# Forming every weight's low part on VectorE instead of sharing the work with GpSimd

## The chip, the cores and the metric

The kernel runs on one core of a Trainium2 chip. The metric is the device time of one execution in microseconds (us); of several executions the median is taken. The names in the profile are PE (TensorE, matrix products), PEld (its weight loads), DVE (VectorE), ACT (ScalarE), POOL (GpSimd) and SP (SyncE, which issues the weight transfers).

## The reference

Two layers of a hybrid diffusion backbone run over 256 latent and 256 context tokens of width 1024. Cut to what matters:

```python
for l in range(2):
    xn, hn = adaln(x, norm1[l], ...), adaln(h, norm1[l], ...)      # latent, context
    u = [xn; hn] @ w_in[l]                     # one projection, feeds three mixers
    ya = latent_attention(u); yb = window_attention(u); yc = gated_deltanet(u)
    y = merge(gates, ya @ w_a, yb @ w_b, yc @ w_c) @ w_out[l]
    x = x + m[2] * y
    a, b = split(dwconv(adaln(x, norm2[l], ...) @ ffn_up[l], ffn_conv[l]))
    x = x + m[5] * ((silu(a) * b) @ ffn_down[l])
    # the context stream h likewise, in layer 0 only: the last layer drops it after the mixers
out = rmsnorm(x, norm_f)
```

All inputs and outputs are fp32.

## The kernel before

**Products in three parts.** Each fp32 product is made of three reduced-precision (fp32r) products. A weight tile comes as `raw` from HBM; ACT casts it to the high part `wh` (line 194), and the low part `wl = raw - wh` is formed by a subtraction (`split_L`, line 184). `mm3` (lines 204 to 206) then adds `wh*xh`, `wh*xl` and `wl*xh` in PSUM. So the product of line 206 is the first that needs `wl`. Activations are split in the same way by `split` (ACT cast, line 199; DVE subtraction, line 200).

**Tiles and buffers.** `linear` goes over units of 256 output columns; each unit takes weight tiles of 128 x 1024 (four blocks of 128 rows by 256 columns; 128 x 768 at the end of `ffn_down`). There are three `raw`, three `wh` and four `wl` buffers. PSUM tiles are tagged `mm` (three) and `g` (five). With both streams a product has 512 columns, in the last layer after the mixers 256.

**Who forms `wl`.** `split_L` adds a share `lpool` to a running sum and gives the subtraction to GpSimd each time the sum reaches 1, else to VectorE. `lpool` is 1.0 from the first weights to the end of layer 0's first projections, 0 in the DeltaNet stages, and 0.33 from the attentions through the merges, the output projection and the feed-forwards. So there GpSimd forms each third low part.

**Other work on the two engines.** In a feed-forward, each pair of 128-wide blocks goes: ACT scales the product (1606), DVE adds the two shifted terms of the convolution (1609, 1611), ACT applies silu to the first block (1623), POOL multiplies the two (1627), and `split` makes the parts that `ffn_down` reads (199, 200). Residuals are added by DVE (1566). A norm squares on ACT (368), sums on POOL (or DVE at the end, 372), sums over partitions on PE (383), takes the power -1/2 on POOL (348), spreads it on PE (391) and scales on DVE and ACT (404, 410, 411).

**Order.** Each engine and each DMA queue runs its own instructions in order. The order is made when the program is built, by a scheduler that takes the instructions by priority and by readiness under its own costs; semaphores are added by it. The kernel steers it with generators (`run_gen`, `fill`), which interleave projections with the DeltaNet chain.

Of the kernel before, what the change touches and what calls it, by code (L numbers as in the profile page):

```python
# [5 lines left out]
F32 = mybir.dt.float32  # L6
# [3 lines left out]
ALU = mybir.AluOpType  # L10
# [19 lines left out]
def make_consts():  # L30
# [56 lines left out]
MARK = None  # L87
P = dict(pw=4,
    l1={}, s2=(2, 1, 2, 0), pe=(0.0, 0.1, 0.0, 0.0), ov=0, np=(0.1, 0.0, 0.25, 0), ly=2, qs=(0, 4), dec1=3.0, dec2=4.0, sol1=4.2, sol2=4.0,
    sol3=1.0, sol4=2.0, sca=(1.0, 2.0), scb=(1.0, 2.0), scc=(1.0, 2.0), lpg=0.0, lpn=0.33, cap=12.0, sl=(0.3, 0.3, 0.5, 0.1), modc=(4.0, 0.9),  # L90
    lag=(0, 0, 2, 4, 5), nmod=(2, 5), hk=(5, 12), f0=(1.0, 1.6, 1.0, 1.0, 1.5, 1.0, 1.0), f1=(1.0, 1.0, 1.0, 0.3, 1.0, 1.0, 0.3), lat=1.0,
    bx=4, wd=0, dc=1, gk=(0, 0), hpe=60, w_t=5, w_k=3, w_s=0, w_r=1.5, w_n=3, w_o=4.0, nr=3, nh=3, nl=4, nb2=7, st=0, ab=(0.0, 0.0, 0.0, 0.0),
    st2=6, lp0=1.0, lpb=0.33, bge=2, hpa=40, hpn=0, hpk=40, hpv=40)

_INS = ["x", "c", "ctx", "c_ctx", "w_mod", "b_mod", "norm1", "norm2", "w_in", "mla_q_norm", "mla_kv_norm",
        "w_uq", "w_ukv", "swa_sink", "gdn_conv", "gdn_a_log", "gdn_dt_bias", "gdn_norm",
# [38 lines left out]
class Kernel:  # L135
# [40 lines left out]

    def split_L(self, out, x, h):

        self.lacc += self.lpool
        e = self.nc.vector  # L180
        if self.lacc >= 1.0:
            self.lacc -= 1.0
            e = self.nc.gpsimd
        e.tensor_tensor(out=out, in0=x, in1=h.bitcast(F32), op=ALU.subtract)  # L184

    def load_split(self, srcs, shape):

# [228 lines left out]
    def setup(self):  # L416
        nc, i = self.nc, self.ins
        self.cst = self.per.tile([128, CONSTS.shape[1]], F32, name="cst")
        nc.sync.dma_start(out=self.cst[:, :130], in_=i["consts"][:, :130])
        ident = self.con("ident")  # L420
        crow, cs = self.b2([16, 128]), self.b2([16, 128])
        nc.scalar.dma_start(out=crow[0:8, :], in_=i["c_ctx"].rearrange("(k p) -> k p", p=128))
        nc.scalar.dma_start(out=crow[8:16, :], in_=i["c"][0].rearrange("(k p) -> k p", p=128))
        self.x0 = [self.b4([128, D]) for _ in range(4)]
        for n in (2, 3, 0, 1):
            nc.sync.dma_start(out=self.x0[n], in_=i["x" if n // 2 else "ctx"][0, n % 2 * 128:n % 2 * 128 + 128, :])
        nc.scalar.activation(out=cs, in_=crow, func=AF.Silu)
        self.cT = self.per.tile([128, KD, 32], F32, name="cT")
        nc.vector.memset(self.cT, 0.0)
        pc = self.ps([128, T], "g")  # L430
        nc.tensor.transpose(pc[:, :16], cs, ident[:16, :16])
        nc.vector.tensor_copy(self.cT[:, :, 0:2].rearrange("p k s -> p s k"), pc[:, :16].rearrange("p (s k) -> p s k", k=KD))
        self.vec, self.fcv, self.mod, self.AB = [], [], [], []
        for l in range(DEPTH):
            self.vec.append(self.per.tile([128, NVEC], F32, name=f"vec{l}"))
            self.fcv.append(self.per.tile([128, FC_ROWS], F32, name=f"fcv{l}"))
            self.mod.append(self.per.tile([128, 6, KD, 2], F32, name=f"mod{l}"))
            self.AB.append(self.per.tile([128, 2, KD, 2], F32, name=f"AB{l}"))
        self.lpool = self.P["lp0"]
        m = self.m0 = self.modulation_first()  # L440
        for _ in range(self.P["st"]):
            next(m)
        v = self.load_vectors(0)
        next(v)
        self.load_x()
        for _ in range(4 - self.P["st"]):
            next(m)
        next(v)
        next(m)
        self.v0 = v  # L450
# [848 lines left out]
    def layer(self, l):  # L1299
# [89 lines left out]
        def finish(*gens):  # L1389
            self.gsync()  # L1390
            self.finish(*gens)
# [12 lines left out]

        self.XT, self.N, self.qk, self.oacc, self.qr, self.St = {}, {}, {}, {}, {}, None
        self.mark(f"gproj_{l}")
        if l:
            self.lpool = self.P["lpg"]
        self.gdn_alloc()
        self.gates = gates() if self.P["gk"][l] else None  # L1410
        self.run_gen(self.gdn_part(l, X, 1, lambda: self.norm1(l, 1)))
# [6 lines left out]
        mods = [self.modulation(l, 1), self.modulation(l, 2)]  # L1418
        self.gates = self.gates or gates()
        self.queue = [gq, gv, gkv, self.gates]  # L1420
        self.lpool = self.P["lpg"]
        spill = self.dram.tile([128, KD, T], F32, name=f"spill{l}")
        for j in range(2):
            nc.sync.dma_start(out=spill[:, j * 4:j * 4 + 4], in_=self.xT[j])
# [30 lines left out]
        chain(go1)  # L1455
        self.mark(f"mlaprep_{l}")
        finish(gsq, gmq)
        self.lpool = self.P["lpn"]
        yc = A["zs"]
        qh, kh, vt = A["qh"], A["kh"], A["vt"]  # L1460
        self.mark(f"mla_{l}")
# [117 lines left out]
                self.mod_A(l, 1)  # L1579
            yield from self.norm_mod(xT, self.AB[l][:, 1], self.mod[l][:, 3], *self.X2, s)  # L1580

        self.lpool = self.P["lpb"]
        self.run_gen(self.linear(i["w_out"][l], 0, KD, 0, D, (mH, mL), residual(2, 0, True), cols=lambda _: slice(0, n),
                                 split=None if last else 3, hook=lambda: norm2(0)))
        if last:
# [10 lines left out]
        for half in range(2):  # L1596
            aH, aL = [], []
            for a in (aH, aL):
                for al, m_ in ((self.s8, 4), (self.s8, 4), (self.b4, 2), (self.b4, 1)):
                    t = al([128, m_, T], F32R)  # L1600
                    a += [t[:, k] for k in range(m_)]
            f0 = half * 11

            def conv(y, p, cs, o):
                c0, c1 = cs.start // S, cs.stop // S
                nc.scalar.activation(out=y[:, cs], in_=p[:, cs], func=AF.Identity, scale=fc[:, 44 + o:45 + o])
                yv = y.rearrange("p (s j) -> p s j", s=2)[:, c0:c1]
                pv = p.rearrange("p (s j) -> p s j", s=2)[:, c0:c1]
                nc.vector.scalar_tensor_tensor(out=yv[:, :, 1:], in0=pv[:, :, :S - 1], scalar=fc[:, o:o + 1],
                                               in1=yv[:, :, 1:], op0=ALU.mult, op1=ALU.add)  # L1610
                nc.vector.scalar_tensor_tensor(out=yv[:, :, :S - 1], in0=pv[:, :, 1:], scalar=fc[:, 88 + o:89 + o],  # L1611
                                               in1=yv[:, :, :S - 1], op0=ALU.mult, op1=ALU.add)
                return y

            for f in range(f0, f0 + 11, 2):
                nf = min(2, f0 + 11 - f)
                av = {}

                def eva(t, p, cs):
                    if t not in av:  # L1620
                        av[t] = self.b2([128, T])
                    y = conv(av[t], p, cs, f + t)
                    nc.scalar.activation(out=y[:, cs], in_=y[:, cs], func=AF.Silu)

                def evb(t, p, cs):
                    y = conv(self.b2([128, T]), p, cs, f + t + 22)
                    nc.gpsimd.tensor_tensor(out=y[:, cs], in0=y[:, cs], in1=av[t][:, cs], op=ALU.mult)  # L1627
                    self.split(aH[f + t - f0][:, cs], aL[f + t - f0][:, cs], y[:, cs])

                if nf == 1:  # L1630
                    self.run_gen(self.linear(i["ffn_up"][l], 0, KD, (f * 128, (f + 22) * 128), 256, X,
                                             lambda t, p, cs: evb(0, p, cs) if t else eva(0, p, cs), cols=c_o))
                    continue
                self.run_gen(self.linear(i["ffn_up"][l], 0, KD, f * 128, nf * 128, X, eva, cols=c_o,
                                         split=0 if f == 0 and not last else None, hook=lambda: norm2(1)))
                self.lpool = self.P["lpn"]
                self.run_gen(self.linear(i["ffn_up"][l], 0, KD, (f + 22) * 128, nf * 128, X, evb, cols=c_o))
            if last and half:
                self.final_load()
            self.lpool = self.P["lpb"] if half else self.P["lpn"]  # L1640
            self.run_gen(self.linear(i["ffn_down"][l], f0, 11, 0, D, (aH, aL), residual(5, None, half == 1), cols=c_o,
                                     split=3 if half == 1 and not last else None, hook=lambda: self.norm1(l + 1, 0)))
        while self.bg:
# [10 lines left out]
    def run(self):  # L1654
        nc, tc, i = self.nc, self.tc, self.ins
        self.NS8, self.NS4, self.NB2, self.NSM = 8, 9, self.P["nb2"], 32
        self.NRAW, self.NWH, self.NWL, self.NMM = self.P["nr"], self.P["nh"], self.P["nl"], 3
        self.lpool, self.lacc = 0.0, 0.0
        self.queue, self.bg, self.gcount, self.bg_every, self.credit, self.modcost, self.gates, self.wait, self.sq_last, self.bgx, self.unit, self.wide = [], [], 0, 3, 0.0, 4.0, None, 0.0, None, None, 0, False
        with tc.tile_pool(name="per", bufs=1) as self.per, tc.tile_pool(name="sb", bufs=1) as self.pool, \  # L1660
                tc.tile_pool(name="psum", bufs=1, space=PSUM) as self.psum, \
                tc.tile_pool(name="dram", bufs=1, space=DRAM) as self.dram:
            self.setup()
            for l in range(DEPTH):
                self.layer(l)
            self.mark("final")
            self.final()
# [62 lines left out]
```

## Time and profile before

| | us |
|---|---|
| median of 3 runs | 1794.27 |
| lowest and highest | 1787.89, 1797.77 |
| the profiled execution | 1803.63 |
| its span, first to last instruction | 1801.8 |

The profiled execution lies 9.4 us above the median, and 1.8 us of it lie outside the span. The mean granted clock of TensorE over the span is 0.962 of full speed. In the rows, times are us from the span's start unless marked ns; `x` is a count; a bracket or the last column tells how long the engine had been idle and what ended the wait.

### The profile page before, as it was taken

How to read it: one execution, taken by the hardware profiler on the slowest of the kernel's cores; microseconds unless marked ns; L12 is line 12 of the kernel's file. 1: busy time of each engine (PE TensorE's matmuls, PEld its weight loads, DVE VectorE, ACT ScalarE, POOL GpSimd, SP SyncE). 2: the span in 40 equal slices, each digit the busy share in tenths (PEclk: the TensorE clock that was granted, in tenths of full speed). 3: DMA queues.
4: the chain of work that ended last, by engine and by line, in shares of the span. 5: the costliest groups of instructions: out<-in, count | busy, mean ns of one | idle time of the engine just before them, and what ended most of it. 6: DMA issues, size and time to landing. Idle time of an engine off the chain costs nothing. (4 is left out here: it accounts for less than half of the span.)

```text
span 1801.8 us, 31553 instructions
## 1 busy us (share of the span) xinstructions
PE 1689.5 (94%) x12723; PEld 1371.2 (76%) x12723; DVE 1082.6 (60%) x2089; ACT 767.2 (43%) x1371; POOL 456.0 (25%) x351
## 2 busy tenths in 40 slices
PE   7989888999999999999999999989889899999997
PEld 4768766776557888668888888768777668989996
DVE  2896594565775433445334434798886866466573
ACT  3644411234665233334324333565433564554453
POOL 3130501122100423112212222032412403434241
PEclk9999997998999999999999999999989899989998
DMA  9323325333134543853333345334441214745553
GB/s 341 114 80 108 96 88 164 68 85 101 45 117 155 184 136 109 311 170 94 97 103 93 94 155 155 94 88 131 100 100 30 81 59 138 239 122 169 182 171 111
DMA packets 216944, 228.75 MB, mean 127 GB/s; under 512 B 51228, under 2 KB 195422, under 8 KB 215646
## 3 DMA queue, kind: packets, MB, share of 16 engines
q1 hardware_dynamic: 211582, 220.11, 39.9%
q10 hardware_dynamic: 4928, 6.56, 1.0%
q8 instruction: 100, 1.64, 0.4%
q14 instruction: 46, 0.38, 0.1%
q0 software_dynamic: 288, 0.06, 0.0%
HBM read 213.85 MB, written 11.80 MB: 125 GB/s over the span
## 5 line engine op out<-in xcount | busy, mean ns | idle before, releaser
L194 ACT CAST wh<-raw 128x1024 fp32r<-128x1024 f32 (+2 forms) x294 | 298.4, 1016 | 412.8 <-PE mm L205 212.8
L184 DVE TENSOR_TENSOR wl<-raw,wh 128x1024 fp32r<-128x1024 f32 (+1 forms) x224 | 280.3, 1252 | 201.9 <-ACT wh L194 182.3
L204 PE MATMUL mm<-xnh,wh 128*128 128x512 f32 (+2 forms) x1072 | 381.6, 357 | 5.6 <-ACT wh L194 2.4
L206 PE MATMUL mm<-xnh,wl 128*128 128x512 f32 (+2 forms) x1072 | 376.1, 353 | 2.6 <-DVE wl L184 1.3
L205 PE MATMUL mm<-xnl,wh 128*128 128x512 f32 (+2 forms) x1072 | 375.5, 351 | 0.7 <-DVE xnl L411 0.6
L184 POOL TENSOR_TENSOR wl<-raw,wh 128x1024 fp32r<-128x1024 f32 (+2 forms) x70 | 162.5, 2322 | 448.7 <-ACT wh L194 419.2
L204 PEld LDWEIGHTS mm<-xnh,wh 128*128 128x128 f32 (+1 forms) x1072 | 206.4, 193 | 39.6 <-issue 7.6
L206 PEld LDWEIGHTS mm<-xnh,wl 128*128 128x128 f32 (+1 forms) x1072 | 205.7, 192 | 33.1 <-issue 2.9
L205 PEld LDWEIGHTS mm<-xnl,wh 128*128 128x128 f32 (+1 forms) x1072 | 206.4, 193 | 28.1 <-DVE xnl L411 2.2
L204 PE MATMUL g<-xnh,wh 128*128 128x256 f32 (+1 forms) x496 | 167.9, 340 | 1.4 <-ACT xnh L410 1.4
L206 PE MATMUL g<-xnh,wl 128*128 128x256 f32 (+1 forms) x496 | 166.6, 337 | 2.1 <-POOL wl L184 2.1
L205 PE MATMUL g<-xnl,wh 128*128 128x256 f32 (+1 forms) x496 | 166.3, 337 | 0.2 <-DVE xnl L411 0.2
L204 PE MATMUL mm<-s,wh 128*128 128x256 f32 (+1 forms) x458 | 151.0, 331 | 2.3 <-ACT s L199 1.7
L206 PE MATMUL mm<-s,wl 128*128 128x256 f32 (+1 forms) x458 | 150.8, 330 | 1.7 <-POOL wl L184 1.1
L205 PE MATMUL mm<-s,wh 128*128 128x256 f32 (+1 forms) x458 | 150.5, 329 | 0.1
L204 PEld LDWEIGHTS g<-xnh,wh 128*128 128x128 f32 x496 | 94.7, 192 | 15.4 <-issue 3.7
L205 PE MATMUL g<-s,wh 128*128 128x512 f32 (+1 forms) x304 | 103.6, 341 | 2.4 <-DVE s L200 2.4
L204 PE MATMUL g<-s,wh 128*128 128x512 f32 (+1 forms) x304 | 104.1, 342 | 1.3 <-ACT s L199 1.3
L206 PEld LDWEIGHTS g<-xnh,wl 128*128 128x128 f32 x496 | 94.6, 191 | 13.2 <-POOL wl L184 2.9
L206 PE MATMUL g<-s,wl 128*128 128x512 f32 (+1 forms) x304 | 103.3, 340 | 0.0
L205 PEld LDWEIGHTS g<-xnl,wh 128*128 128x128 f32 x496 | 94.8, 192 | 10.0 <-DVE xnl L411 0.8
L1627 POOL TENSOR_TENSOR b<-b,b 128x512 f32<-128x512 f32 (+1 forms) x44 | 54.6, 1240 | 170.9 <-DVE b L1611 149.6
(286 smaller groups left out, 2865.9 us busy)
## 6 DMA issues: line engine op xcount, KB each, us to landing
raw<-in_w_in_dram SPq DMA_DIRECT2D x92, 512.0 KB
raw<-in_ffn_up_dram SPq DMA_DIRECT2D x80, 512.0 KB
s<-in_w_mod_dram SPq DMA_DIRECT2D x64, 512.0 KB
raw<-in_w_mod_dram SPq DMA_DIRECT2D x32, 512.0 KB
raw<-in_ffn_down_dram SPq DMA_DIRECT2D x32, 512.0 KB
raw<-in_w_out_dram SPq DMA_DIRECT2D x16, 512.0 KB
raw<-in_ffn_down_dram SPq DMA_DIRECT2D x16, 384.0 KB
spill<-s SPq DMA_DIRECT2D x4, 1024.0 KB
```

The source lines that it names most:

```text
L184: e.tensor_tensor(out=out, in0=x, in1=h.bitcast(F32), op=ALU.subtract)
L194: nc.scalar.copy(H, raw)
L204: mm(ps, lhsT=wH, rhs=xH, start=start, stop=False)
L205: mm(ps, lhsT=wH, rhs=xL, start=False, stop=False)
L206: mm(ps, lhsT=wL, rhs=xH, start=False, stop=stop)
L1627: nc.gpsimd.tensor_tensor(out=y[:, cs], in0=y[:, cs], in1=av[t][:, cs], op=ALU.mult)
```

## The change

`split_L` always takes VectorE, and the shares and their running sum are gone. Nothing else is edited. The diff, without the lines of the parameter table:

```diff
     def split_L(self, out, x, h):
 
-        self.lacc += self.lpool
-        e = self.nc.vector
-        if self.lacc >= 1.0:
-            self.lacc -= 1.0
-            e = self.nc.gpsimd
-        e.tensor_tensor(out=out, in0=x, in1=h.bitcast(F32), op=ALU.subtract)
+        self.nc.vector.tensor_tensor(out=out, in0=x, in1=h.bitcast(F32), op=ALU.subtract)
...
-        self.lpool = self.P["lp0"]        # setup: 1.0
-        if l:
-            self.lpool = self.P["lpg"]    # gproj of layer 1: 0.0
-        self.lpool = self.P["lpg"]        # after the first projections: 0.0
-        self.lpool = self.P["lpn"]        # attentions, merges: 0.33
-        self.lpool = self.P["lpb"]        # output projection: 0.33
-                self.lpool = self.P["lpn"]
-            self.lpool = self.P["lpb"] if half else self.P["lpn"]
-        self.lpool, self.lacc = 0.0, 0.0
```

## Rows read from the trace of the kernel before

**Rows 1.** The page's first part: busy time, share of the span, instructions

```profile
PE 1689.5 (94%) x12723; PEld 1371.2 (76%) x12723; DVE 1082.6 (60%) x2089; ACT 767.2 (43%) x1371; POOL 456.0 (25%) x351
```

**Rows 2.** Instructions grouped by line: busy us, mean ns, idle before and its releasers

```profile
L184 POOL TENSOR_TENSOR wl<-raw,wh 128x1024 fp32r<-128x1024 f32 (+2 forms) x70 | 162.5, 2322 | 448.7 <-ACT wh L194 419.2 <-DVE s L1566 13.3 <-PE g L206 11.8
```

**Rows 3.** Busy time by stretch: PE, PEld, DVE, ACT, POOL, clock, DMA share, GB/s

```profile
760.00:1125.00 365.00, 361.91 (x1767) 295.91 (x1766) 155.96 (x213) 128.13 (x176) 87.17 (x55) 1.00 0.39 123
...
1590.00:1665.00 75.00, 70.16 (x560) 68.69 (x560) 52.16 (x76) 40.74 (x69) 33.08 (x19) 0.98 0.52 158
...
1700.00:1770.00 70.00, 66.16 (x525) 65.56 (x524) 49.42 (x68) 36.65 (x66) 28.60 (x18) 0.95 0.58 176
```

**Rows 4.** The same stretches, line 184 alone: DVE busy, POOL busy, clock

```profile
1500.00:1590.00 90.00, 23.35 (x17) 21.54 (x9) 0.94 0.58 184
1590.00:1665.00 75.00, 19.67 (x17) 19.17 (x8) 0.98 0.52 158
...
1700.00:1770.00 70.00, 18.37 (x15) 16.77 (x7) 0.95 0.58 176
```

**Rows 5.** PE's waits, 1500 to 1802 us: total us, times, longest

```profile
PE g L206 <- POOL wl L184: 2.1, 3, 0.8
...
PE mm L206 <- POOL wl L184: 1.8, 2, 1.1
```

**Rows 6.** PE's waits, 540 to 1125 us

```profile
PE mm L206 <- POOL wl L184: 0.5, 1, 0.5
```

**Rows 7.** PE's timeline, last layer: start, us, instruction, wait ended

```profile
1579.07 1.22 PE L391 MATMUL g<-cst,sm 128*128 128x128 f32 x4 [1.89 <-POOL sm L348]
...
1655.13 0.39 PE L206 MATMUL mm<-s,wl 128*128 128x256 f32 x1 [1.05 <-POOL wl L184]
1660.41 0.39 PE L204 MATMUL mm<-s,wh 128*128 128x256 f32 x1 [1.66 <-ACT s L199]
...
1761.99 0.58 PE L205 MATMUL g<-s,wh 128*128 128x256 f32 x1 [1.77 <-DVE s L200]
```

**Rows 8.** DVE's timeline: first norm, last norm, the last layer's feed-forward

```profile
44.04 2.32 DVE L411 SCALAR_TENSOR_TENSOR xnl<-b,mod,xnh 128x256 fp32r<-128x256 f32 x3
...
1577.22 0.16 DVE L347 TENSOR_SCALAR sm<-g 128x2 f32<-128x2 f32 x1 [1.62 <-PE g L383]
...
1653.20 2.15 DVE L200 TENSOR_TENSOR s<-b,s 128x256 fp32r<-128x256 f32 x1 [1.38 <-ACT s L199]
...
1658.11 1.22 DVE L184 TENSOR_TENSOR wl<-raw,wh 128x1024 fp32r<-128x1024 f32 x1
1660.39 0.42 DVE L200 TENSOR_TENSOR s<-b,s 128x256 fp32r<-128x256 f32 x1 [1.05 <-ACT s L199]
```

**Rows 9.** POOL's timeline: last norm, and the last layer's feed-forward

```profile
1575.99 2.34 POOL L184 TENSOR_TENSOR wl<-raw,wh 128x1024 fp32r<-128x1024 f32 x1 [4.01 <-ACT wh L194]
1578.30 0.72 POOL L348 TENSOR_TENSOR sm<-sm,cst 128x2 f32<-128x2 f32 x1
...
1658.35 1.57 POOL L1627 TENSOR_TENSOR b<-b,b 128x256 f32<-128x256 f32 x1 [3.28 <-DVE b L1611]
...
1758.62 0.72 POOL L1627 TENSOR_TENSOR b<-b,b 128x256 f32<-128x256 f32 x1 [3.80 <-DVE b L1611]
1759.30 2.35 POOL L184 TENSOR_TENSOR wl<-raw,wh 128x1024 fp32r<-128x1024 f32 x1
```

**Rows 10.** DVE's groups by shape, 1590 to 1770 us

```profile
L184 DVE TENSOR_TENSOR wl<-raw,wh 128x1024 fp32r<-128x1024 f32 x34 | 42.4, 1246 | 18.6 <-ACT wh L194 18.6
L200 DVE TENSOR_TENSOR s<-b,s 128x256 fp32r<-128x256 f32 x22 | 25.0, 1135 | 24.0 <-ACT s L199 24.0
```

**Rows 11.** POOL's groups by shape, 1590 to 1770 us

```profile
L1627 POOL TENSOR_TENSOR b<-b,b 128x256 f32<-128x256 f32 x22 | 26.2, 1191 | 72.4 <-DVE b L1611 67.0 <-ACT wh L194 5.4
```

**Rows 12.** Busy time in stretches of 10 us, columns as in rows 3

```profile
1660.00:1670.00 10.00, 9.52 (x65) 9.32 (x66) 3.95 (x5) 3.54 (x5) 2.39 (x1) 0.83 0.44 146
...
1760.00:1770.00 10.00, 8.23 (x45) 8.03 (x46) 5.76 (x7) 2.97 (x7) 1.66 (x1) 0.66 0.61 196
```

More of the change, by code (lines that the diff above doesn't have):

```diff
@@ L89 @@
     l1={}, s2=(2, 1, 2, 0), pe=(0.0, 0.1, 0.0, 0.0), ov=0, np=(0.1, 0.0, 0.25, 0), ly=2, qs=(0, 4), dec1=3.0, dec2=4.0, sol1=4.2, sol2=4.0,
-    sol3=1.0, sol4=2.0, sca=(1.0, 2.0), scb=(1.0, 2.0), scc=(1.0, 2.0), lpg=0.0, lpn=0.33, cap=12.0, sl=(0.3, 0.3, 0.5, 0.1), modc=(4.0, 0.9),
+    sol3=1.0, sol4=2.0, sca=(1.0, 2.0), scb=(1.0, 2.0), scc=(1.0, 2.0),   cap=12.0, sl=(0.3, 0.3, 0.5, 0.1), modc=(4.0, 0.9),
     lag=(0, 0, 2, 4, 5), nmod=(2, 5), hk=(5, 12), f0=(1.0, 1.6, 1.0, 1.0, 1.5, 1.0, 1.0), f1=(1.0, 1.0, 1.0, 0.3, 1.0, 1.0, 0.3), lat=1.0,
     bx=4, wd=0, dc=1, gk=(0, 0), hpe=60, w_t=5, w_k=3, w_s=0, w_r=1.5, w_n=3, w_o=4.0, nr=3, nh=3, nl=4, nb2=7, st=0, ab=(0.0, 0.0, 0.0, 0.0),
-    st2=6, lp0=1.0, lpb=0.33, bge=2, hpa=40, hpn=0, hpk=40, hpv=40)
+    st2=6, bge=2, hpa=40, hpn=0, hpk=40, hpv=40)
 _INS = ["x", "c", "ctx", "c_ctx", "w_mod", "b_mod", "norm1", "norm2", "w_in", "mla_q_norm", "mla_kv_norm",
```

## The prediction

> **What bounds the kernel now.** I read the page's busy shares first, then the busy time by stretch, then what ended PE's waits, and last the timelines of DVE and POOL around those waits. PE is busy 94% of the span [rows 1], so the subtractions matter only where PE stands idle. POOL forms 70 low parts at 2.322 us each on average [rows 2]; DVE's take 1.246 [rows 10]. By stretch: in layer 0's feed-forward PE works 361.91 of 365 us [rows 3], and over layer 0's attentions, merges and feed-forward together just 0.5 us of PE's waits ended with a low part of POOL [rows 6]. Nothing is to be had there. The last layer is different, because its products have 256 columns and use up a weight tile in half the time: PE is idle 4.84 us in its first feed-forward half and 3.84 us in the second [rows 3]. Of the 70 low parts, 9, 8 and 7 fall into the merges with the output projection and into the two halves [rows 4]. The reader is to see that PE's waits in this layer name POOL, or name something that POOL held up.
>
> **What the change removes.** Five terms, all in the last layer but half a microsecond.
>
> 1. PE waits that end with POOL's low part: 2.1 us in three waits and 1.8 in two [rows 5], and 0.5 in layer 0 [rows 6]: 4.4 us. The longest is 1.05 us [rows 7]; a subtraction of 1.23 us in place of one of about 2.4 would be ready 1.15 us earlier if it starts at the same moment, so I take all of it.
>
> 2. A DVE instruction held by POOL. Line 200 forms an activation's low part. Alone it takes 0.42 us; at 1653.20 it took 2.15 [rows 8]. It reads two SBUF tiles, as POOL's subtraction does. In the second half PE waited 1.77 us for such an instruction at 1761.99 [rows 7], and POOL's subtraction of 2.35 us had begun at 1759.30 [rows 9], so it ended at 1761.65. Without it line 200 is done 1.7 us earlier: 1.7 us.
>
> 3. The first half ends with a wait of 1.66 us at 1660.41, for the cast of an activation [rows 7]. That cast follows POOL's product, which follows DVE's convolution, which stood behind the 2.15 us instruction at 1653.20 [rows 8]. Of its 1.73 us of excess I credit 1.6 to this wait.
>
> 4. The last norm. DVE's line 347 ends at 1577.38 [rows 8]; POOL's power (line 348) begins at 1578.30 because POOL is in a low part from 1575.99 to 1578.33 [rows 9]. PE waited 1.89 us for it [rows 7]. The power can start 0.9 us earlier: 0.9 us.
>
> 5. The clock. After the waits at 1655 and 1660 the granted clock was 0.83 over 10 us, after the wait at 1762 it was 0.66 [rows 12]. Where PE has work, such a stretch costs 10 us times the missing share: 1.7 us and 3.4 us. In the first place the change takes away both waits, so I count 1.7. In the second, 3.84 us of idle PE [rows 3] less the 1.77 and a POOL wait of at most 0.8 [rows 5] leave some 1.3 us of waits, so I count nothing and keep 3.4 as the far end of the gain.
>
> Sum: 4.4 + 1.7 + 1.6 + 0.9 + 1.7 = 10.3 us.
>
> **What it adds.** DVE gets 70 subtractions. In the two halves it is 15 times 1.23 us [rows 4, 8], 18.5 us. But line 200 also loses its excess there: 22 times (1.135 - 0.42) us [rows 8, 10], 15.7 us. So DVE's busy time grows by 2.8 us, from 101.6 of 145 us [rows 3] to 104.4, or from 70% to 72%. Throughput is no limit. What can cost is the order: DVE runs in order, and a subtraction stands ahead of convolutions that clear PSUM, and waits for its cast. For 34 of DVE's own it idled 18.6 us for the cast [rows 10], 0.55 each, so a moved subtraction that is exposed in full costs 1.23 + 0.55 = 1.78 us. Lower bound: none exposed, 0 us, since in the last layer no PE wait ended with a low part made by DVE (the answer behind rows 5 has no such row). Upper bound: all 24 of rows 4, 43 us. I take under two exposures, 3 us, near the lower end, because DVE already forms two thirds of the low parts in the same code without one.
>
> The other places I cost at nothing. In layer 0's feed-forward DVE is busy 156 of 365 us and PE's work covers the rest [rows 3]; without that cover each would cost the 1.78 us again. In the first norm the three instructions at 44.04 took 2.32 us [rows 8] beside a low part of POOL, and in their place DVE gets that subtraction itself: between 1 us of gain and two subtractions in front of the norm, 2.5 us of loss. No transfer is moved and no instruction that issues one; `raw` is freed about 1.2 us earlier, so SP's next weight transfer can start earlier. With the DMA engines busy 52% and 58% in the two halves [rows 3] I see no collision.
>
> So 10.3 - 3 = 7.3 us less. The profiled execution took 1803.63 us, 9.4 above the median of the runs; I take the saving off both: 1796.3 against the former, 1787 against the median of 1794.27.
>
> **A rule against it.** The contention has a second side. Line 1627, POOL's product of two blocks, took 0.72 us at 1758.62 but 1.57 at 1658.35 [rows 9], where DVE's subtraction had begun at 1658.11 [rows 8]; its mean over 22 is 1.191 [rows 11]. The Trainium skill (SBUF — State Buffer, Who interferes with whom) says that a VectorE instruction with two SBUF inputs and a GpSimd instruction that reads SBUF share a read interface, and that whichever starts first keeps it for the whole instruction. The trace agrees on both sides: 2.15 against 0.42 us on DVE, 1.57 against 0.72 on POOL. By this rule the change turns the blocking round instead of ending it, and the sum would be what the second rival gives.
>
> **The rivals.**
>
> *The clock stays up as well.* If the wait at 1762 goes and the clock does not fall to 0.66 behind it, 3.4 us more are won, and with no exposed subtraction it is 13.7 us: 1780.6. For it: the larger of the two waits there goes. Against: the 1.3 us of waits that stay in this half.
>
> *The blocking is turned round.* Line 200's excess of 15.7 us at 1.73 each makes 9 places where POOL blocked DVE. If in all nine a subtraction on DVE now blocks line 1627 instead, at 0.85 us, and PE feels each, 7.7 us come back: -10.3 + 7.7 + 3 = +0.4, or 1794.7. For it: some 12 of the 22 are already stretched (22 times 0.47 us of mean excess, over 0.85). Against: of these stretched products only the one at the end of the first half shows in a PE wait, at 1660.41 [rows 7].
>
> *DVE's queue becomes late.* The place is the last layer's merges and halves, the price 1.78 us for each exposed subtraction. From 6 of the 24 on it eats the gain, from 11 it makes the kernel over 0.5% slower; with 12, 21.4 - 10.3 = +11.1 us, 1805.4. For it: DVE stands in order and its work there is at 70%; the program's order is made anew. Against: no DVE low part ended a PE wait there so far.
>
> **How the numbers follow.** A measurement of this kernel can tell about 0.5%, 9 us, from no change. Chances: forecast 0.43 (its own range 1782 to 1792), clock as well 0.13, turned round 0.25, late queue 0.19. Faster by over 0.5% means below 1785.3: the clock case and two fifths of the forecast, 0.30. Slower means above 1803.2: the late queue, 0.19. Within it: 0.51. The range goes from just below the clock case, 1779, to the lower half of the late queue, 1805, and leaves out some 0.14. The unknown costs lie inside it: 0 to 43 us of exposure weighed by these chances, -1 to +2.5 at the start.
>
> **What would show it.** Right, if line 200's mean in the last halves is near 0.45 us; if no wait of PE names POOL's line 184 and none DVE's takes its place; if line 348 starts within 0.1 us of line 347's end; if the clock around the end of the first half stays at 1. Line 1627's mean should rise above 1.191 us, which costs nothing unless PE waits for the casts behind it. Wrong, if PE waits name DVE's line 184 or convolutions that stand behind it, if the idle time of PE in layer 0 or in the DeltaNet stages changes by several microseconds through the new order, or if the waits in the last layer go and the clock's loss moves elsewhere.

## The result, and the profile after

The changed kernel takes 1780.07 us (median of 4 runs, 1776.76 to 1782.09), the kernel before 1794.5 beside it (1787.89 to 1797.77). The ratio is 0.9891, 95% interval 0.9855 to 0.9926, so 13 to 26 us less. The forecast was 1787.0: the direction was right, and 7.3 us less was forecast where 14.4 came by the medians and 19.6 by the ratio. Over the experiments the kernel before had medians of 1798.02 (17 runs), 1800.42 and 1799.91 (29 runs each), 18 to 20 us above the changed kernel, so the four runs at 1794.5 lie low and the larger figure is nearer. The profiled execution took 1780.76 us, its span 1779.0, with a mean granted clock of 0.968.

Busy time on the page, beside [rows 1], and the low parts that were in [rows 2], now all on VectorE. Line numbers of the changed kernel are 5 to 14 lower, so the subtraction is line 179:

```profile
PE 1679.0 (94%) x12723; PEld 1363.7 (77%) x12723; DVE 1133.4 (64%) x2159; ACT 769.2 (43%) x1371; POOL 300.4 (17%) x281
...
L179 DVE TENSOR_TENSOR wl<-raw,wh 128x1024 fp32r<-128x1024 f32 (+2 forms) x294 | 364.3, 1239 | 250.2 <-ACT wh L189 248.6
```

VectorE has 51 us more and GpSimd 156 us less. What PE waited for in the last layer, 1500 us to the end, beside [rows 5]:

```profile
PE g L1669 <- DVE s L1556: 1.1, 2, 0.6
PE g L199 <- ACT xnh L405: 1.1, 1, 1.1
PE g L386 <- POOL sm L343: 1.1, 1, 1.1
PE g L378 <- DVE b L367: 0.9, 1, 0.9
PE g L378 <- ACT b L363: 0.3, 1, 0.3
```

No row names a low part, a split or a cast of an activation. These 4.5 us are the last norm and the residuals at the end. The stretches of the feed-forward, beside [rows 3, 12] (busy PE, PEld, DVE, ACT, POOL; granted clock; DMA):

```profile
1570.00:1580.00 10.00, 7.83 (x44) 7.45 (x45) 6.44 (x16) 2.85 (x7) 0.73 (x1) 0.66 0.25 78
...
1580.00:1745.00 165.00, 164.89 (x1370) 164.26 (x1368) 123.60 (x181) 95.07 (x151) 25.13 (x22) 1.00 0.59 181
```

PE is idle for 0.11 of 165 us there, and the clock is at its upper level throughout. The groups by shape in the feed-forward, beside [rows 10, 11]:

```profile
L195 DVE TENSOR_TENSOR s<-b,s 128x256 fp32r<-128x256 f32 x22 | 9.2, 419 | 10.7 <-ACT s L194 10.7
...
L1616 POOL TENSOR_TENSOR b<-b,b 128x256 f32<-128x256 f32 x22 | 25.1, 1142 | 142.6 <-DVE b L1600 114.6 <-ACT wh L189 24.5 <-ACT b L1595 3.5
```

Line 195 (line 200 before) takes 0.419 us on average where it took 1.135. The norm, beside [rows 7, 8, 9]:

```profile
1570.69 0.16 DVE L342 TENSOR_SCALAR sm<-g 128x2 f32<-128x2 f32 x1
1570.92 0.73 POOL L343 TENSOR_TENSOR sm<-sm,cst 128x2 f32<-128x2 f32 x1 [5.38 <-DVE sm L342]
1571.70 1.23 PE L386 MATMUL g<-cst,sm 128*128 128x128 f32 x4 [1.06 <-POOL sm L343]
```

The power starts 0.07 us after line 342 ends, and PE's wait for it is 1.06 us, from 1.89.

**Where the time came from.** Two stretches, read from the first and last start of PE's lines in each profile. *Attention* is from the last product of line 1213 to the last of line 1254 (second layer, line numbers of before); *feed-forward* from the last norm's spreading (line 391) to the first transposes of the output (line 1683).

| profile of | attention, us | feed-forward, us |
|---|---|---|
| before | 30.1 | 185.7 |
| changed | 25.3 | 171.4 |
| only the last feed-forward's low parts moved | 28.6 | 170.2 |
| only the second attention's one low part moved | 25.7 | 183.5 |
| only the first norm's six moved | 29.3 | 185.5 |
| all moved but the first norm's six | 25.6 | 171.3 |

The feed-forward gives some 14 us, the attention some 4; the attention alone varies by 1.5 us among the profiles in which its low part wasn't moved. (The two spans differ by 22.8 us, more than the medians do, because the execution of before that was profiled lies 9.4 us above its median.)

### The profile page after: what moved, and what is told of

Its sections match the earlier page's. It is cut to its first block, busy times and chain, and to the rows that moved or that the text cites. A ratio compares the mean times of both kernels' runs of the same rounds, so it can differ in the third digit from the quotient of the medians.

```text
span 1779.0 us, 31557 instructions
## 1 busy us (share of the span) xinstructions
PE 1679.0 (94%) x12723; PEld 1363.7 (77%) x12723; DVE 1133.4 (64%) x2159; ACT 769.2 (43%) x1371; POOL 300.4 (17%) x281
## 5 line engine op out<-in xcount | busy, mean ns | idle before, releaser
L179 DVE TENSOR_TENSOR wl<-raw,wh 128x1024 fp32r<-128x1024 f32 (+2 forms) x294 | 364.3, 1239 | 250.2 <-ACT wh L189 248.6
L200 PEld LDWEIGHTS g<-xnl,wh 128*128 128x128 f32 x496 | 94.7, 191 | 10.1 <-DVE xnl L406 0.8
L199 PEld LDWEIGHTS mm<-s,wh 128*128 128x128 f32 x458 | 87.2, 191 | 8.8 <-DVE s L534 1.1
```

Of the source, the lines that this page charges most:

```text
L179: self.nc.vector.tensor_tensor(out=out, in0=x, in1=h.bitcast(F32), op=ALU.subtract)
L199: mm(ps, lhsT=wH, rhs=xH, start=start, stop=False)
L200: mm(ps, lhsT=wH, rhs=xL, start=False, stop=False)
```

## The experiments

The two theories at the outset. **Held:** a low part on GpSimd holds VectorE's instructions that read two SBUF tiles until it ends; the change ends that. **Late:** the low parts themselves are merely late on GpSimd (2.3 us against 1.25, behind its other work), or its products stand behind them. A third possibility is that the program's new **order** is better by itself. Each ratio below is a run's time over that of the kernel before, executed beside it.

**One set of low parts at a time.** The kernel before, with GpSimd left out in one stage (the name that each stage has in the code); the other sets differ only in the names:

```diff
         if self.lacc >= 1.0:
             self.lacc -= 1.0
-            e = self.nc.gpsimd
+            if not self.stage.startswith(("ffn_1",)):     # the last feed-forward
+                e = self.nc.gpsimd
```

> Only the 22 low parts that GpSimd forms in the last layer's feed-forward go to VectorE; all else as in the kernel before. PE's and SP's queues are the same, word for word, as before. Theory 'held' (GpSimd's subtractions hold VectorE's two-input instructions and come late themselves, and PE's waits and the clock's falls in this stage follow from it): the stretch from the last norm to the end is 13 to 16 us shorter than in the profile of before, no wait of PE names line 184's subtraction or line 200, the clock stays at 1.00 at the ends of both halves; time 0.990 to 0.994 of before. Theory 'order' (the newly made order of the whole program gains, wherever it comes from): under 4 us, as the order of the other stages is not touched.

1781.91 us, ratio 0.9905 (0.9880 to 0.9930). These 22 low parts bring nearly all of it. The instructions of TensorE and of the queue that issues the weights stand in the same order as in the kernel before, so a better order of products or transfers isn't needed for it. ScalarE's and VectorE's don't: some casts and sums of this stage stand earlier or later around the moved low parts. That a better order on these two engines helps is ruled out only by the runs with idle work below, which leave both in place.

> The kernel before, with the one low part of the second layer's attention that GpSimd forms given to VectorE (all others stay). If that one low part held VectorE's sums at 1413 us, for which TensorE waited 2.48 us there, and let the clock fall to 0.69 to 0.83 for some 30 us: 1 to 5 us faster, the three sums of line 1244 take 1.3 us together and not 3.3, and the PE wait there falls from 2.5 to 0.5 us. If the attention of the changed kernel is shorter for another reason (what came ahead of it, the clock): 0, within 1 us.

1795.33 us, ratio 0.9978 (0.9958 to 0.9998): 4 us (0.4 to 7.5), from a single low part. The timelines of VectorE, GpSimd and PE, before:

```profile
1413.28 3.34 DVE L1244 TENSOR_TENSOR s<-b,b 32x256 f32<-32x256 f32 x3
1413.32 2.59 POOL L184 TENSOR_TENSOR wl<-raw,wh 128x1024 fp32r<-128x1024 f32 x1
1416.65 0.42 DVE L1256 TENSOR_TENSOR b<-g,cst 128x256 f32<-128x256 f32 x1
...
1417.13 1.22 PE L1254 MATMUL g<-s,cst 128*128 128x256 f32 x2 [2.48 <-DVE b L1256]
```

and with that low part on VectorE:

```profile
1411.90 1.28 DVE L1249 TENSOR_TENSOR s<-b,b 32x256 f32<-32x256 f32 x3
1413.21 0.42 DVE L1261 TENSOR_TENSOR b<-g,cst 128x256 f32<-128x256 f32 x1
1413.55 1.22 DVE L189 TENSOR_TENSOR wl<-raw,wh 128x1024 fp32r<-128x1024 f32 x1
...
1413.69 0.70 PE L1259 MATMUL g<-s,cst 128*128 128x256 f32 x2 [0.42 <-DVE b L1261]
```

Three sums of the rotated queries (line 1244) stretched from 1.28 to 3.34 us beside GpSimd's subtraction, and line 1256 behind them, which frees PE's PSUM tile, came 2.06 us later. Formed by VectorE, the subtraction simply goes behind line 1256. The granted clock from 1410 to 1420 and from 1420 to 1430 us, 0.82 and 0.83 in the profile of before, is 1.00 in both here: the 4 us hold the wait and the clock behind it.

> The kernel before, with only the first norm's six low parts given to VectorE. The changed kernel has its first tables 1.9 us later than the kernel before, and 0.9 to 1.5 us of that are still there through the first layer. If the six low parts in VectorE's queue are the cause: 1 to 2.5 us slower. If the six gain what the sum of line 411 lost beside GpSimd (2.32 us at 44 us): 0 to 1 us faster.

1800.35 us, ratio 1.0001 (0.9983 to 1.0020). No loss and no gain. The profile after has its first tables 1.9 us later than before (line 777 there, at 86.1 and 84.2 us), but so has the profile with only the last feed-forward changed (85.9), where nothing differs at the start: executions differ by that much, and the expected cause falls.

> All as in the changed kernel, but the six low parts of the first norm stay on GpSimd. In the changed profile the DeltaNet tables start 1.9 us later than before. Theory 'held': these 1.9 us come back and the rest of the gain stays: 1 to 3 us under the changed kernel, 0.987 to 0.990 of before. Theory 'order': the 1.9 us are a chance of the order and no difference to the changed kernel of a set sign.

1777.28 us, ratio 0.9889 (0.9860 to 0.9919), the changed kernel's 0.9891 again. Both runs say that the first six are worth nothing that can be told.

> The kernel before, with only the low parts of the first layer that GpSimd forms (attention, merge, feed-forward, and the norm that follows) given to VectorE. If what the low parts cost GpSimd's neighbour is only seen where TensorE has no other work to go on with: 0, within 3 us, since the trace of before shows PE waits on POOL of some 0.5 us in that layer. If it is worth per low part what it is in the last feed-forward: 5 to 17 us faster.

1798.22 us, ratio 0.9995 (0.9977 to 1.0013): nothing, with the same low parts in the same code as in the last layer. So in the first layer, where a unit's products have 512 columns, what the low parts hold up or bring late is covered.

> The kernel before, with only the low parts of the second layer's merges and of the norm behind them that GpSimd forms given to VectorE. If the low part at 1576 us delayed the norm's power (line 348, 0.72 us late, and the clock at 0.66 from 1570 to 1580): 0.5 to 3 us faster. If that is hidden behind the feed-forward's first weights: 0.

1798.23 us, ratio 0.9993 (0.9975 to 1.0012): not distinguishable from none. It doesn't test the norm's power, for which it was meant: the low part that is in the way at 1576 us belongs to the feed-forward's first weights. PE's wait for the power is 2.0 us in this kernel, and 1.1 in the one with only the feed-forward moved.

Together the five sets that were moved alone give 0.0095 + 0.0022 - 0.0001 + 0.0005 + 0.0007 = 0.0128, and the change 0.0109 (0.0074 to 0.0145).

**Put back what GpSimd did, and nothing else.** The changed kernel, with idle work on GpSimd at the 22 places of the last feed-forward where a low part stood. Nobody waits for this work. The instructions of TensorE, VectorE, ScalarE and the issuing queue are those of the changed kernel, in its order. First, a subtraction that reads `wh` twice into a dead region of the constants:

```diff
+            if self.stage.startswith("ffn_1"):            # at the 22 places
+                self.nc.gpsimd.tensor_tensor(out=self.idle(n), in0=h.bitcast(F32), in1=h.bitcast(F32), op=ALU.subtract)
         e.tensor_tensor(out=out, in0=x, in1=h.bitcast(F32), op=ALU.subtract)    # e is VectorE
```

> The changed kernel, and in the last layer's feed-forward GpSimd also makes 22 subtractions of the same size at the places where it formed low parts before; they read wh twice, write over constants that nothing reads any more, and nobody waits for the result. The queues of PE, VectorE, ScalarE and SyncE are the same as in the changed kernel. Theory 'held': the activations' low parts are stretched to about 2.1 us again in about 9 of 22, and 5 to 12 us of the gain are lost against the changed kernel, with the clock falling at the end of a half. Theory 'late' (the gain is only that VectorE's low part is ready 1.2 us sooner): within 3 us of the changed kernel.

1797.23 us, ratio 0.9986 (0.9968 to 1.0004): the whole gain is gone, though no low part is formed by GpSimd. Groups by shape on VectorE and GpSimd from 1580 to 1770 us, and PE's waits:

```profile
L210 DVE TENSOR_TENSOR s<-b,s 128x256 fp32r<-128x256 f32 x22 | 21.4, 972 | 20.2 <-ACT s L209 20.2
```

```profile
L189 POOL TENSOR_TENSOR cst<-wh 128x1024 f32<-128x1024 f32 x21 | 51.7, 2462 | 50.8 <-ACT wh L204 50.8
```

```profile
PE mm L216 <- DVE wl L190: 3.1, 3, 1.5
...
PE mm L214 <- ACT s L209: 2.3, 1, 2.3
PE g L214 <- ACT s L209: 2.3, 1, 2.3
PE g L216 <- DVE wl L190: 2.3, 5, 0.7
PE g L215 <- DVE s L210: 1.3, 1, 1.3
```

PE waits for VectorE's own low parts now, and for casts that stand behind held sums. So a late low part of GpSimd isn't needed for the loss. But GpSimd was also taken for 2.5 us each time, and `wh` was held longer.

> As the idle reads, but each of the 22 is two memsets of 128 x 1024 over the same unused constants: GpSimd's queue is as full, but it reads no SBUF. Theory 'held': the activations' low parts stay at 0.42 us and the time is within 3 us of the changed kernel. If instead a full queue of GpSimd is the cause (its product of the two blocks stands behind other work): 4 us or more are lost, as with the idle reads.

1781.06 us, ratio 0.9899 (0.9874 to 0.9924). The two memsets at each place (line 190, 1 us each) cost nothing. This control is weak: the memsets wait for nothing, and the scheduler put them much earlier, in the attention, so GpSimd wasn't taken at the 22 places. The next two runs mend it: a copy of one column of `wh` goes first, so that the work behind it waits for the cast as a low part did.

```diff
+                self.nc.gpsimd.tensor_copy(self.idle(1)[:, :, 0:1], h.bitcast(F32)[:, 0:1, 0:1])
+                for _ in range(2):                                     # writes only
+                    self.nc.gpsimd.memset(self.idle(4), 0.0)
...
+                # in its place in the second kernel: reads two inputs of the dead region
+                self.nc.gpsimd.tensor_tensor(out=self.idle(4), in0=self.idle(4), in1=self.idle(4), op=ALU.subtract)
```

> The changed kernel, with idle work on GpSimd at the 22 places of the last feed-forward where a low part stood: a copy of one column of wh, which keeps the wait for ScalarE's cast, and then two memsets of 1 us each, which read nothing. GpSimd is so taken for about 2.1 us at each place, as by the low parts of the kernel before (2.34 us), and its own later work (the product of line 1637, line 1627 of the kernel before) stands behind it. If it is GpSimd's reading that holds VectorE: within 3 us of the changed kernel (1778 to 1784), the mean of the sums of line 210 (line 200 before) stays below 0.6 us, and no PE wait of 2 us names VectorE's low part. If it is that GpSimd is taken, and its products come late behind the idle work: at least 6 us of the 14 to 17 lost again (1787 or more), with waits on GpSimd's products.

> As the run with memsets, at the same 22 places and with the same copy of one column ahead of it, but the idle work is one subtraction of two inputs from a region that nobody uses (4 x 256 columns, written back to the same place). It takes about 2.3 us, and holds none of the buffers that the weights' low parts use. If GpSimd's reading holds VectorE whatever it reads: most of the gain lost again, 1789 to 1798, the mean of line 210 above 0.75 us, PE waits on VectorE's low part. If the loss of the earlier run with idle reads came from wh being held longer, or from GpSimd's queue: within 3 us of the changed kernel, or equal to the run with memsets.

Memsets: 1781.28 us, ratio 0.9898 (0.9869 to 0.9927), the gain stays. Subtractions: 1798.13 us, ratio 0.9988 (0.9971 to 1.0006), it is gone. With memsets, GpSimd's timeline and VectorE's at one place, and the stretch from 1580 to 1770 us:

```profile
1607.93 1.97 POOL L190 MEMSET cst<- 128x1024 f32 x2
...
1608.21 0.42 DVE L211 TENSOR_TENSOR s<-b,s 128x256 fp32r<-128x256 f32 x1 [1.07 <-ACT s L210]
```

```profile
1580.00:1770.00 190.00, 189.26 (x1567) 188.01 (x1566) 134.75 (x199) 103.39 (x168) 88.22 (x85) 1.00 0.55 170
```

With subtractions, the same place and the same stretch:

```profile
1605.64 1.90 POOL L189 TENSOR_TENSOR cst<-cst 128x1024 f32<-128x1024 f32 x1
...
1605.90 1.91 DVE L210 TENSOR_TENSOR s<-b,s 128x256 fp32r<-128x256 f32 x1 [1.07 <-ACT s L209]
```

```profile
1580.00:1770.00 190.00, 179.18 (x1426) 176.31 (x1425) 144.66 (x188) 96.06 (x157) 86.45 (x62) 0.96 0.55 167
```

GpSimd is as busy in both, 88.2 and 86.5 us, at the same places, with the same waits. In both, the idle work starts some 0.27 us before the sum of `split`. Beside memsets the sum takes 0.42 us; beside the subtraction it ends 0.27 us after GpSimd's does. So the loss in these runs isn't that GpSimd is taken or that its products are late, and not which buffer it reads: its reading is what costs. PE's busy time in the stretch falls by 10.1 us, and the clock is at 0.66 in two slices of 10 us (from 1650 and from 1750), which at 0.34 each is 6.8 us: 16.9 together. From the last norm's spreading to the first transposes the two profiles differ by 16.3 us (187.7 and 171.4), and the medians by 16.85.

The sums of `split` aren't all that is held: VectorE's low parts read two SBUF tiles too. Their means beside the subtractions, and then beside the memsets:

```profile
L190 DVE TENSOR_TENSOR wl<-raw,wh 128x1024 fp32r<-128x1024 f32 x54 | 75.0, 1388 | 18.3 <-ACT wh L204 18.2
```

```profile
L191 DVE TENSOR_TENSOR wl<-raw,wh 128x1024 fp32r<-128x1024 f32 x57 | 71.7, 1258 | 29.2 <-ACT wh L205 28.5
```

That is some 7 us of holds on top of those of the sums, and PE waits 4.1 us in all for low parts of VectorE beside the subtractions, and not at all beside the memsets. In the kernel before, VectorE's low parts were hardly held (1.246 us [rows 10]), while GpSimd's own were late (3.9 us of PE's waits [rows 5]). So the run shows that holds alone can cost the whole gain; it doesn't show how the loss of the kernel before divides between holds and late low parts.

**How much reading.** The same, with a copy of the dead region onto itself (one input) in place of the subtraction:

```diff
-                self.nc.gpsimd.tensor_tensor(out=self.idle(4), in0=self.idle(4), in1=self.idle(4), op=ALU.subtract)
+                self.nc.gpsimd.tensor_copy(self.idle(4), self.idle(4))
```

> As the two runs before it (a copy of one column of wh, then idle work on GpSimd, at the 22 places of the last feed-forward; the queues of the other engines are the changed kernel's), but the idle work is a copy with one input, of 4 x 256 columns of the unused region onto itself. With memsets, which read nothing, the gain stayed (1781.3); with a subtraction of two inputs it was lost (1798.1). If any wide reading by GpSimd holds VectorE: 1789 or more, the mean of line 210 above 0.7 us. If it takes two inputs: 1777 to 1785, line 210 below 0.5 us. In between, 1783 to 1789, if VectorE and GpSimd share something by turns and one input takes half of it.

1781.52 us, ratio 0.9892 (0.9867 to 0.9918): the time is that expected if it takes two inputs to hold VectorE. The rows say otherwise. GpSimd's and VectorE's timeline at one place, then VectorE's and GpSimd's groups:

```profile
1609.55 1.05 POOL L189 COPY cst<-cst 128x1024 f32<-128x1024 f32 x1
...
1609.83 1.04 DVE L210 TENSOR_TENSOR s<-b,s 128x256 fp32r<-128x256 f32 x1 [1.07 <-ACT s L209]
```

```profile
L210 DVE TENSOR_TENSOR s<-b,s 128x256 fp32r<-128x256 f32 x22 | 11.1, 503 | 10.7 <-ACT s L209 10.7
```

```profile
L189 POOL COPY cst<-cst 128x1024 f32<-128x1024 f32 x21 | 24.4, 1161 | 1.3
```

A one-input copy holds the sum too, until it ends, but that is after 1.05 us. Three of the 22 sums were held, by 0.62 us each; beside the subtractions six were, by 1.5 us each. The mean of 0.503 lies nearer to the expected 0.5 than to 0.7, and yet it is three held and nineteen free. Two of the short holds were covered. After the third, at 1645.01, PE waits once, until 1650.94, for the cast of an activation, where the changed kernel has no such wait; the medians can't tell what that costs:

```profile
PE mm L214 <- ACT s L209: 1.4, 1, 1.4
```

**How much cover VectorE has.** The changed kernel, with each of the 22 low parts formed twice by VectorE, into the same place:

```diff
+            if self.stage.startswith("ffn_1"):            # at the 22 places
+                e.tensor_tensor(out=out, in0=x, in1=h.bitcast(F32), op=ALU.subtract)
         e.tensor_tensor(out=out, in0=x, in1=h.bitcast(F32), op=ALU.subtract)
```

> The changed kernel, with each of the 22 low parts of the last feed-forward that moved formed twice by VectorE, into the same place: 22 x 1.27 = 28 us more on VectorE, which is busy for 123.6 of the 165 us from 1580 to 1745. The forecast counted 3 us for low parts that come in ahead of a sum of line 200, and bounded them at 0 and 43. If VectorE's slack covers such work, as the changed kernel's trace says (no PE wait names a low part): within 3 us of the changed kernel even so (1777 to 1784), VectorE at some 152 of 165 us. If the cover is nearly used up: 5 to 25 us slower than the changed kernel (1785 to 1805), with PE waits on VectorE's low parts and on the sums, as the forecast's bound of 1.78 us each would have it (39 us at most).

1793.81 us, ratio 0.9959 (0.9940 to 0.9978). That is 0.0068 of the time, some 12 us, or 0.56 us for each. PE's waits and the same stretch:

```profile
PE mm L215 <- DVE wl L189: 3.4, 5, 1.3
PE g L215 <- DVE wl L189: 3.1, 4, 1.3
```

```profile
1580.00:1770.00 190.00, 180.93 (x1476) 177.73 (x1475) 147.60 (x211) 99.31 (x162) 29.80 (x22) 1.00 0.55 169
```

VectorE is busy for 147.6 of 190 us, and waits appear all the same: the slack by busy share says little. One subtraction more at each of the places is covered, a second isn't: PE waits nine times for a low part, for 1.3 us at most. PE's busy time is 8.3 us less than with memsets. The scheduler changed the order in this kernel (six of PE's products, at 1591 to 1595 us, and casts and sums on ScalarE and VectorE in the whole stage), so that the doubling isn't all that differs.

## Why the prediction was right in direction and short in size

**What failed is the sum, not its mechanism.** Four terms were mis-sized or missing: the second stretch of the clock in term 5 (3.4 us, counted as nothing), a wait of 1.3 us beside it that was taken to stay, the exposure (3 us were charged and none came), and the attention (some 4 us, in no term). With them 7.3 becomes 7.3 + 3.4 + 1.3 + 3 + 4 = 19.0, beside the 19.6 of the ratio. The two agree better than the interval of 13 to 26 allows one to claim.

**The mechanism** of terms 1 to 3 is shown as a whole. Line 200's mean fell to 0.419 us (0.45 was forecast), the waits on GpSimd's low parts and behind held sums are all gone, and putting GpSimd's reads back restores waits behind held VectorE instructions and the time. How much of term 1 is the low parts' own lateness wasn't separated.

**Term 4**, the last norm, was sized rightly: 0.9 us was forecast, and PE's wait fell from 1.89 to 1.06.

**Term 5, the clock, was mis-sized.** The second place, 3.4 us, was counted as nothing, on the argument that 1.3 us of waits would stay in that half and let the clock fall. It was a wait of 1.30 us at 1759.84, for a cast of line 199, which was in no term. The trace of before shows what it hung on:

```profile
1750.00 2.18 DVE L200 TENSOR_TENSOR s<-b,s 128x256 fp32r<-128x256 f32 x1 [1.38 <-ACT s L199]
...
1753.27 1.56 POOL L1627 TENSOR_TENSOR b<-b,b 128x256 f32<-128x256 f32 x1 [1.36 <-DVE b L1611]
1754.86 0.41 ACT L199 CAST s<-b 128x256 fp32r<-128x256 f32 x1 [3.58 <-POOL b L1627]
...
1759.84 0.38 PE L204 MATMUL g<-s,wh 128*128 128x256 f32 x1 [1.30 <-ACT s L199]
```

GpSimd was in a low part from 1749.49 to 1751.90, so the sum at 1750.00 took 2.18 us; the convolution, the product and the cast behind it came late. VectorE took that cast's sum at 1755.30 and then ran without a pause up to the next pair's product and cast, for which PE waited. It is much the chain of term 3 a second time, so this wait hung on a held sum as well and went with it. In the stretch from 1590 to 1770 of before PE was idle for 8.7 us and the clock cost 1.7 + 3.4; that is 13.8 us, and the feed-forward became 14.3 us shorter. The rival *the clock stays up as well* is what happened, and it had been given 0.13. That its 1780.6 lies so near to 1780.07 is luck: it has neither the 1.3 us nor the attention, and the median of 1794.27 that it starts from is low.

**The exposure, 3 us, was nothing.** No PE wait in the last layer names a low part of VectorE. The doubled run shows how near that was: an exposed subtraction has a price, 0.56 us on average there, from the second one on. The upper bound was counted short: the rows behind "all 24" leave out 1665 to 1700 us and what comes after 1770, where GpSimd forms 4 and 2 more low parts.

**The attention was missed.** "All in the last layer but half a microsecond" rested on PE's waits from 540 to 1125 and from 1500 to the end. The stretch between holds a held sum that costs 4 us (0.4 to 7.5), by the run that moves one low part. It can't be found under GpSimd's name: PE's wait of 2.5 us there is put down to VectorE's line 1256. With the feed-forward's 14.3 it makes 18.3 of the 19.6 us that the ratio gives.

**The rivals that fell.** *Blocking turned round:* VectorE's subtractions do stretch GpSimd's product, but no more than before (line 1616 at 1.142 us, against 1.191; forecast was a rise), and in the profile with only the last feed-forward moved the same product took 0.814 on average with the same time, so a product held by 0.3 us on average changes nothing there. *Late queue:* it needs six exposed subtractions and there was none.

**The first norm and layer 0** were costed at nothing, and runs say 1.0001 and 0.9995.

## What to carry to other kernels

When an engine on the side is slow, look for what it holds up on others: list the instructions of one form with their durations, and take those far above the shortest (0.42 against 2.15 us) to the timeline of the other engine. The wait that costs is put down to the held engine or to one behind it, so a search for the slow engine's name in the waits finds part of it: here 3.9 us in the last layer, against 7.3 in four others that went or nearly went (1.8, 1.7 and 1.3 in the feed-forward, 2.5 in the attention). Sum the idle time of the stretch and the clock's loss behind it as one term, since they go together when all of the waits have one cause; and read the waits of every stretch, not only of those where the moved work is dense.

## What the runs showed of the hardware

GpSimd's work on 128 x 1024 took 0.96 us on average as a memset, 1.16 as a copy and 2.04 as a subtraction, and it holds a VectorE instruction with two SBUF inputs in the last two cases until 0.27 us after its own end, not in the first. A VectorE instruction that takes one of its inputs from PSUM wasn't held, as two rows of the changed kernel's attention show, with GpSimd multiplying and adding two SBUF tiles meanwhile:

```profile
1417.46 2.50 POOL L1252 TENSOR_TENSOR s<-s,b 128x256 f32<-128x256 f32 x2 [1.20 <-DVE b L1250]
1417.63 0.42 DVE L1250 TENSOR_TENSOR b<-g,cst 128x256 f32<-128x256 f32 x1
```

The Trainium skill (SBUF — State Buffer, Who interferes with whom) says that two SBUF inputs on VectorE contend with a GpSimd instruction that reads SBUF, and not with one that only writes. The memsets and the subtractions agree with it, at 0.42 and 1.91 us, and so does the one-input copy, at 1.04. By that rule the change could have turned the blocking round, as the second rival had it; the runs show that both sides block. In the kernel before, products of GpSimd that took 1.57 and 1.56 us beside a subtraction of VectorE stood in two of the chains that PE waited for; in the changed kernel 10 of the 22 are stretched (12 before), and PE waits behind none.

Three held sums of 0.62 us cost nothing that the medians can tell, and six of 1.5 us, with some 7 us of holds on VectorE's low parts, cost 17 us: between them lies the cover that the program's order happens to leave, and the clock's fall to 0.66 behind the longest waits takes 6.8 of the 17.
